# A two-layer encoder on one core: bias expanded within the second stage, one weight sum on VectorE, token sums in the slot freed last

## The chip, the core and the metric

The kernel runs on one core of a Trainium2 chip. Its engines are TensorE (PE; its weight loads are shown apart, as PEld), VectorE (DVE), ScalarE (ACT), GpSimd (POOL) and SyncE (SP), which here issues nearly all DMAs. The metric is the device time of one execution in microseconds; before the change it is 1210.97 us, the median of 3 runs (1210.27 to 1211.98).

## The reference

An encoder trunk of two layers over 512 tokens (8 rows of 64) of width 1024, all in float32. Each layer is an attention and a squared-ReLU MLP with 4096 hidden columns, with a normalisation ahead of each; a last normalisation ends it. The first layer's attention is a hybrid of two kinds; the second's looks at a neighbourhood of 8 x 16 positions and adds a learned bias by relative position. What the change touches:

```
def sq_relu_mlp(h, w_up, w_down):
    u = jax.nn.relu(h @ w_up)
    return (u * u) @ w_down

# in neighbourhood_attention, for a block of 128 queries:
bias = rpb[:, rblk, cblk].astype(jnp.float32)
sc = jnp.einsum('bhqd,bhqkd->bhqk', qblk, kg).astype(jnp.float32) * scale + bias[None]
```

## The kernel before

**Precision.** A float32 factor is split into a high part (rounded by a copy to a narrower float type, on ACT) and a low part (what is left, by a subtraction on DVE). A product is three matmuls: high by high, high by low, low by high.

**The MLP of layer 0** (`mlp`, L1201 on) goes through the 32 tiles of 128 hidden columns in three stages, z = 0, 1, 2: up product of some tiles, squared ReLU, then down product of these tiles, added to the residual `hT` (L1199). The first 6 hidden tiles are made by a plain up product. The rest are made *by sevens* (class `Seven`): two by two blocks of weights and of tokens are multiplied with seven products in place of eight, from sums and differences of blocks. The last 12 tiles of the third stage are kept raw, without a split, as their down product is done by sevens as well (`u7`): it needs sums of token blocks (`Seven.sums`, L325 to L327 on POOL) and splits of these sums (`Seven.split`, L348 on ACT and L349 on DVE). These run, a step at a time, between the matmuls of the third stage's plain down product. `u7` then makes four groups of two output tiles (L1226 adds each to `hT`), with six weight chunks each.

**A weight chunk by sevens** (`seven_chunk`, L289 on) is a 128 x 1024 tile `raw` with four blocks loaded by one DMA of SP (L292), 256 KB. POOL forms three more: L294 (one block of 128 x 128), L295 (two) and L296 (one, from an output of L295). ACT makes the high parts of seven blocks (L299, `whi`) and DVE the low parts (L300, `wlo`). PE then does 21 matmuls (L373 to L375). There are four `raw` buffers and three each of `whi` and `wlo`. At the end of a pair of output tiles L382 to L385 put the sums together on DVE. Layer 0 has 76 such chunks: 16 in the second stage, 36 in the third (the last 24 for the twelve raw tiles) and 24 in `u7`. Plain products have weight chunks of their own (`chunk`), with L211 on ACT and L201 on DVE.

**The order of the work.** Chunks are asked for by `plan` and made by `weights`, two ahead of the one that PE works on (`AHEAD = 2`). In the attention the order of the instructions is written out by hand; in the MLP a scheduler orders each engine's instructions as the program is built, and each engine, SP's queue of DMAs among them, then runs its own in that order, waiting where an operand is late.

**Slots.** Token tiles live in a fixed set of 128 x 1024 slots (class `Slot`, L65); a new one takes the slot at the head of the list of free ones, and a slot that is given up goes to its end.

**The bias** (L1236 to L1258) stands behind `mlp(0)` in the source. Eight small DMAs bring the rows of the table into the slot R (L1242); POOL fills and copies them into Fi and Fe (L1244 to L1248); 48 DMAs of 64 or 128 KB write the expanded bias to DRAM (`bx`, L1251, L1254 and L1255). Layer 1's attention reads it back.

Of the kernel before, what the change touches and what calls it, by code (L numbers as in the profile page):

```python
# [8 lines left out]
F32 = mybir.dt.float32  # L9
F32R = mybir.dt.float32r  # L10
I32 = mybir.dt.int32
AF = mybir.ActivationFunctionType
ALU = mybir.AluOpType
# [5 lines left out]
P = 128  # L19
# [3 lines left out]
NEG = -1e30  # L23
# [12 lines left out]
def encoder_kernel(ctx: ExitStack, tc: tile.TileContext, ins, out, dbg=None):  # L36
    nc = tc.nc
    PE, ACT, DVE, POOL, SP = nc.tensor, nc.scalar, nc.vector, nc.gpsimd, nc.sync
# [7 lines left out]
    dr = ctx.enter_context(tc.tile_pool(name="dr", bufs=1, space=bass.MemoryType.DRAM))  # L46
# [16 lines left out]
        return f"{s}_{cnt[0]}"  # L63

    class Slot:  # L65
        def __init__(self, dt=F32R):
            self.i = take()[0]
            self.t = big.tile([P, 1024], dt, tag=f"a{self.i}", name=nm("a"))

# [162 lines left out]
    def plan(*spec, make=None):  # L232
        asked.append((make or chunk, spec))
        return len(asked) - 1
# [51 lines left out]

    SEVEN = [(0, 0), (2, 2), (4, 5), (3, 3), (5, 4), (6, 1), (1, 6)]

    def seven_chunk(w, k0, c0):  # L289

        raw = wp.tile([P, 1024], F32, tag="raw", bufs=4, name=nm("raw"))
        SP.dma_start(raw[:, 0:512].rearrange("p (k n) -> p k n", k=2), rows(w, k0, 2)[:, :, c0 : c0 + 256])  # L292
        r = raw.rearrange("p (b n) -> p b n", n=P)
        POOL.tensor_tensor(r[:, 6], r[:, 0], r[:, 1], op=ALU.subtract)  # L294
        POOL.tensor_tensor(r[:, 4:6], r[:, 2:3].to_broadcast([P, 2, P]), r[:, 0:7:6], op=ALU.add)  # L295
        POOL.tensor_tensor(r[:, 7], r[:, 3], r[:, 5], op=ALU.subtract)  # L296
        hi = wp.tile([P, 1024], F32R, tag="whi", name=nm("whi"))
        lo = wp.tile([P, 1024], F32R, tag="wlo", name=nm("wlo"))
        ACT.activation(hi[:, 0:896], raw[:, 128:1024], AF.Copy)  # L299
        return hi, lo, [lambda: DVE.tensor_tensor(lo[:, 0:896], raw[:, 128:1024], f32(hi[:, 0:896]),  # L300
                                                  op=ALU.subtract)]

    class Seven:
# [13 lines left out]
            q = self.number(kp, b)  # L317
            return self.slots[q // 2].t.rearrange("p (q z n) -> p q z n", q=2, z=2)[:, q % 2]

        def sums(self, kp, raw):  # L320

            t = Slot(F32)
            self.raw[kp] = raw, t
            r, t_ = (s_.t.rearrange("p (b n) -> p b n", n=256) for s_ in (raw, t))
            POOL.tensor_tensor(t_[:, 0:2], r[:, 0:1].to_broadcast([P, 2, 256]), r[:, 1:3], op=ALU.subtract)  # L325
            POOL.tensor_tensor(t_[:, 2], r[:, 2], t_[:, 0], op=ALU.subtract)
            POOL.tensor_tensor(t_[:, 3], r[:, 3], t_[:, 2], op=ALU.subtract)  # L327
# [27 lines left out]
            for s_ in self.slots.values():  # L355
                s_.free()

        def plan(self, w, c0, k0=0):
            return [plan(w, k0 + 2 * kp, c0, make=seven_chunk) for kp in range(self.np)]

        def run(self, ids, evac):

# [726 lines left out]
    def first_product(l):  # L1089

        w = ins["ffn_w_up"][l]
        X = [Slot() for _ in range(KD)]
        acc = pp.tile([P, S], F32, tag="p", name=nm("acc"))
        for k in range(KD):
            split_g(hT[:, k, :], gffn(l, k), X[k].pair())
            sumsq_acc(k, acc, DVE)
        xp = [s_.pair() for s_ in X]
        U, R = [], []
        rb = keep([P, S], F32, "rb")
        state = dict(c=SIZES[l][0], ids=None, plain=False)  # L1100
        x7 = Seven(KD)

        def ev(j, b):
            U.append(Slot())
            t = scratch()
            DVE.scalar_tensor_tensor(t, b, 0.0, rb, op0=ALU.max, op1=ALU.mult)
            uu = scratch()
            ACT.activation(uu, t, AF.Square)
            split(uu, U[-1].pair())

        def norm():
            r = compact_r(acc)
            bk = stb()
            bcast_cols(lambda i: r[:, i : i + 1].to_broadcast([P, P]), P, bk)
            ACT.activation(rb, bk, AF.Copy)

        def x_sums(kp):
            raw = Slot(F32)
            for z in range(2):
                k = 2 * kp + z  # L1120
                DVE.scalar_tensor_tensor(raw.t[:, S * z : S * z + S], hT[:, k, :], gffn(l, k), rb, op0=ALU.mult,
                                         op1=ALU.mult)
            x7.sums(kp, raw)

        def raw_evac(w_):
            ACT.activation(w_.t, w_.t, AF.Relu)
            ACT.activation(w_.t, w_.t, AF.Square)
            R.append(w_)
            return True

        def pair_evac(w_):
            raw_evac(w_)
            R.pop()
            for z in range(2):
                U.append(Slot())
                split(w_.t[:, S * z : S * z + S], U[-1].pair())

        def plain():
            four = product(w, 0, xp, tiles(0, 512), ev, lambda n: [mmb(), mmb(), mmb(), sbk()])
            two = product(w, 0, xp, tiles(512, 256), ev, lambda n: [sbk(), ob()], kstep=4)  # L1140
            for n, _ in enumerate(four):
                if n == (11 if l == 0 else 13):
                    norm()
                if n == 14:
                    x_sums(0)
                    x_sums(1)
            for n, _ in enumerate(two):
                if n == 4:
                    x_sums(2)
                if n == 6:  # L1150
                    x_sums(3)
            flip[0] = 1
            for s_ in X:
                s_.free()
            state["plain"] = True

        def later(c, n):

            if (c, n) in ((0, 2), (0, 10), (0, 18), (1, 4)):
                x7.split({(0, 2): 0, (0, 10): 1, (0, 18): 2, (1, 4): 3}[c, n])  # L1160

        def ahead():
            state["ids"] = x7.plan(w, P * state["c"])

        def stage(n, raw=0):

            if not state["plain"]:
                plain()
            left = n + raw - len(U)
            while left:  # L1170
                i = state["ids"]
                state["c"] += 2
                left -= 2
                if left:
                    ahead()
                for _ in x7.run(i, pair_evac if left >= raw else raw_evac):
                    pass
            if state["c"] == 32:
                x7.free()
            got = list(U), list(R)  # L1180
            U.clear()
            R.clear()
            return got

        return stage, ahead, later

    def mlp(l):


        stage, ahead, later = first_product(l)  # L1190
        w = ins["ffn_w_down"][l]
        k0 = 0
        for z, n in enumerate(SIZES[l][:3]):
            raw = SIZES[l][3] if z == 2 else 0
# [7 lines left out]
            k0 += n  # L1202
            if raw:
                u7 = Seven(raw)
                ids = [u7.plan(w, 256 * m, k0) for m in range(4)]
                u7.sums(0, R[0])
            else:
                ahead()
            every = 8 * n // u7.np if raw else 0
            for c, gen in enumerate(gens):  # L1210
                for i, _ in enumerate(gen):
                    if z == 0:
                        later(c, i)
                    if raw:
                        kp, at = divmod(4 * n * c + i, every)
                        if at == 0 and kp + 1 < u7.np:
                            u7.sums(kp + 1, R[kp + 1])
                        if at == 2 and kp < u7.np:
                            u7.split(kp)
            for s_ in U:  # L1220
# [10 lines left out]

    mlp(0)

    bx = dr.tile([16, 2, P, 256], F32, name="bx")  # L1236
    R = Slot(F32)
    Fi = Slot(F32)
    Fe = Slot(F32)
    rpb = ins["od_rpb"][0]  # L1240
    for qr in range(8):
        SP.dma_start(R.t[16 * qr : 16 * qr + 16, 0:248],  # L1242
                       rpb.rearrange("h a b -> h (a b)")[:, (7 - qr) * 31 : (7 - qr) * 31 + 248])
    POOL.memset(Fi.t[:, 0:376], NEG)  # L1244
    POOL.memset(Fe.t[:, 256:512], NEG)
    rv = R.t[:, 0:248].rearrange("p (k d) -> p d k", d=31)
    POOL.tensor_copy(Fi.t[:, 0:376].rearrange("p (j k) -> p j k", k=8)[:, 15:31, :], rv[:, 7:23, :])
    POOL.tensor_copy(Fe.t[:, 0:248].rearrange("p (j k) -> p j k", k=8), rv)  # L1248
    bxv = bx.rearrange("h t (c r) k -> t c r h k", r=8)
    for c in range(16):  # L1250
        SP.dma_start(bxv[0, c].rearrange("r h k -> r h k"), Fi.t[:, (15 - c) * 8 : (15 - c) * 8 + 256])  # L1251

        v, off = (1, (7 - c) * 8) if c < 8 else (0, (23 - c) * 8)
        SP.dma_start(bxv[1, c][:, :, 128 * v : 128 * v + 128], Fe.t[:, off : off + 128])  # L1254
        SP.dma_start(bxv[1, c][:, :, 128 - 128 * v : 256 - 128 * v], Fe.t[:, 256:384])  # L1255
    R.free()
    Fi.free()
    Fe.free()  # L1258

    X = [Slot() for _ in range(KD)]  # L1260
    acc = pp.tile([P, S], F32, tag="p", name=nm("acc"))
# [423 lines left out]
```

## Time and profile before

| what | value |
| --- | --- |
| median of 3 runs | 1210.97 us (1210.27 to 1211.98) |
| the profiled execution | 1210.45 us |
| its span | 1208.7 us |
| mean granted PE clock | 0.995 |
| DMA packets, MB | 108511, 127.99 |
| mean DMA rate | 106 GB/s |

The span is the time from the first to the last instruction in the profile; the rest of the execution's time lies around it. A group line of the profile names line, engine, operation and tiles, then the number of instructions, their busy time in us and the mean of one in ns, then the time that the engine sat idle just ahead of them and what ended it. A row of the timeline has the start and the duration in us, and in brackets the wait ahead of it and its releaser. A row of a window has its bounds and length, the busy time and number of instructions of each engine, the granted PE clock as a share of the full one, the busy share of the DMA engines and GB/s.

### The profile page before, as it was taken

To read this page: it belongs to the slowest core of one execution; us is meant where nothing else is said; L and a number is where in the kernel's file an instruction comes from. 1 tells how busy PE (TensorE), PEld (TensorE's weight loads), DVE (VectorE), ACT (ScalarE), POOL (GpSimd) and SP (SyncE) were. 2 spreads that over 40 slices of the span, in tenths; PEclk is the share of its full clock that TensorE was granted. 3 is DMA by queue.
4 is the path that set the end of the run, shared out by engine and by line. 5 is a ranking of instruction groups with operands and counts; after the bars stand their busy time and mean duration, and the time that the engine had idled before them with its cause. 6 is when DMAs were issued, how large, how long until landed. Compare 5 with 4: busy or idle time off the path is not lost.

```text
span 1208.7 us, 19500 instructions
## 1 busy us (share of the span) xinstructions
PE 1174.6 (97%) x7020; PEld 1018.2 (84%) x7020; DVE 841.7 (70%) x1447; ACT 629.8 (52%) x1065; POOL 514.1 (43%) x641
## 2 busy tenths in 40 slices
PE   9999999999999999998999999999999999999997
PEld 7667788887898898877998988988878988988985
DVE  4588988878666477794885675767984753664764
ACT  4577677755355156562443555655463642551553
POOL 3257252205472389974941232221343903723800
PEclk9999999999999999999999999999999999999999
DMA  7223314212234133324655564433222341341432
GB/s 239 72 57 90 84 54 130 70 53 77 72 96 149 46 99 94 116 85 131 188 149 145 157 162 133 128 100 121 88 79 62 105 157 44 92 153 44 123 123 69
DMA packets 108511, 127.99 MB, mean 106 GB/s; under 512 B 8979, under 2 KB 83648, under 8 KB 108416
## 3 DMA queue, kind: packets, MB, share of 16 engines
q1 hardware_dynamic: 105360, 119.30, 33.7%
q0 software_dynamic: 2304, 6.31, 2.3%
q10 hardware_dynamic: 752, 1.15, 0.4%
q8 instruction: 55, 0.90, 0.3%
q14 instruction: 40, 0.33, 0.1%
HBM read 104.32 MB, written 6.29 MB: 92 GB/s over the span
## 4 chain that ended last, share of the span: by engine, by line
PE 75%; DVE 8%; POOL 6%; ACT 4%; issue 3%; DMA 2%; SPq 1%; POOLq 0%; DVEq 0%; ACTq 0%
PE mm L486 7%; PE mm L488 7%; PE mm L487 7%; PE s L976 2%; PE o L964 2%; POOL raw L295 2%; PE mm L375 2%; PE mm L373 2%; PE mm L374 2%; PE s L488 2%; PE s L486 2%; PE t L951 2%; PE s L487 2%; PE mm L1583 2%; PE mm L1585 2%
## 5 line engine op out<-in xcount | busy, mean ns | idle before, releaser
L300 DVE TENSOR_TENSOR wlo<-raw,whi 128x896 fp32r<-128x896 f32 x128 | 160.8, 1256 | 122.5 <-ACT whi L299 120.2
L299 ACT ACTIVATE whi<-raw 128x896 fp32r<-128x896 f32 x128 | 121.6, 950 | 199.3 <-POOL raw L296 63.0
L201 DVE TENSOR_TENSOR wlo<-raw,whi 128x1024 fp32r<-128x1024 f32 (+4 forms) x123 | 144.9, 1182 | 97.3 <-ACT whi L211 97.0
L211 ACT ACTIVATE whi<-raw 128x1024 fp32r<-128x1024 f32 (+3 forms) x126 | 122.6, 974 | 126.4 <-PE o L1585 30.6
L294 POOL TENSOR_TENSOR raw<-raw 128x128 f32<-128x128 f32 x128 | 84.3, 659 | 231.4 <-DMA raw<-in_ffn_w_up_dram 153.7
L486 PE MATMUL mm<-a,whi 128*128 128x512 f32 x419 | 169.4, 406 | 0.2 <-DVE hT L910 0.2
L487 PE MATMUL mm<-a,whi 128*128 128x512 f32 x419 | 165.9, 396 | 0.0
L488 PE MATMUL mm<-a,wlo 128*128 128x512 f32 x419 | 165.7, 397 | 0.0
L295 POOL TENSOR_TENSOR raw<-raw 128x256 f32<-128x256 f32 x128 | 120.5, 942 | 10.0
L296 POOL TENSOR_TENSOR raw<-raw 128x128 f32<-128x128 f32 x128 | 105.8, 827 | 10.0
L375 PE MATMUL mm<-a,wlo 128*128 128x256 f32 x340 | 97.9, 288 | 4.7 <-DVE wlo L300 4.6
L373 PE MATMUL mm<-a,whi 128*128 128x256 f32 x340 | 96.5, 284 | 5.4 <-ACT whi L299 5.4
L374 PE MATMUL mm<-a,whi 128*128 128x256 f32 x340 | 96.2, 283 | 0.0
L488 PEld LDWEIGHTS mm<-a,wlo 128*128 128x128 f32 x419 | 78.5, 188 | 19.7 <-issue 1.7
L486 PEld LDWEIGHTS mm<-a,whi 128*128 128x128 f32 x419 | 78.7, 188 | 17.3 <-issue 1.9
L487 PEld LDWEIGHTS mm<-a,whi 128*128 128x128 f32 x419 | 78.9, 188 | 16.3 <-issue 1.7
L984 POOL TENSOR_SCALAR p<-p,ti 128x512 f32<-128x512 f32 x64 | 46.3, 725 | 88.2 <-DVE ti L983 74.0
L1386 POOL TENSOR_SCALAR p<-p,ti 128x256 f32<-128x256 f32 x64 | 35.6, 567 | 105.1 <-DVE ti L1385 92.0
L375 PEld LDWEIGHTS mm<-a,wlo 128*128 128x128 f32 x340 | 65.0, 191 | 7.0 <-DVE wlo L300 6.7
L373 PEld LDWEIGHTS mm<-a,whi 128*128 128x128 f32 x340 | 65.1, 192 | 6.0 <-ACT whi L299 5.8
L374 PE MATMUL t<-a,whi 128*128 128x256 f32 x240 | 67.4, 281 | 0.0
L375 PE MATMUL t<-a,wlo 128*128 128x256 f32 x240 | 67.3, 280 | 0.0
(325 smaller groups left out, 3284.9 us busy)
## 6 DMA issues: line engine op xcount, KB each, us to landing
raw<-in_ffn_w_down_dram SPq DMA_DIRECT2D x52, 512.0 KB
raw<-in_ffn_w_up_dram SPq DMA_DIRECT2D x104, 256.0 KB
raw<-in_od_w_qkv_dram SPq DMA_DIRECT2D x64, 128.0 KB
raw<-in_ffn_w_up_dram SPq DMA_DIRECT2D x12, 512.0 KB
raw<-in_ffn_w_down_dram SPq DMA_DIRECT2D x24, 256.0 KB
raw<-in_ev_w_in_dram SPq DMA_DIRECT2D x12, 384.0 KB
a<-a SPq DMA_DIRECT2D x18, 256.0 KB
bias<-bx SPq DMA_DIRECT2D x16, 256.0 KB
```

The lines of the kernel that those rows point to most:

```text
L201: z = lambda: (eng or DVE).tensor_tensor(to, src, f32(high), op=ALU.subtract)
L211: ACT.activation(hi[:, 0:m], raw[:, 0:m], AF.Copy)
L295: POOL.tensor_tensor(r[:, 4:6], r[:, 2:3].to_broadcast([P, 2, P]), r[:, 0:7:6], op=ALU.add)
L296: POOL.tensor_tensor(r[:, 7], r[:, 3], r[:, 5], op=ALU.subtract)
L299: ACT.activation(hi[:, 0:896], raw[:, 128:1024], AF.Copy)
L300: return hi, lo, [lambda: DVE.tensor_tensor(lo[:, 0:896], raw[:, 128:1024], f32(hi[:, 0:896]), op=ALU.subtract)]
L373: PE.matmul(o, wh, x[:, 0], start=kp == 0 and n in (0, 1, 3, 5), stop=False, skip_group_check=True)
L374: PE.matmul(o, wh, x[:, 1], start=False, stop=False, skip_group_check=True)
L375: PE.matmul(o, wl, x[:, 0], start=False, stop=kp == self.np - 1, skip_group_check=True)
L486: PE.matmul(o, wh, xh, start=first, stop=False)
L487: PE.matmul(o, wh, xl, start=False, stop=False)
L488: PE.matmul(o, wl, xh, start=False, stop=last)
```

## The change

Three edits. First, the bias code becomes a generator, `bias_rows`, with a `yield` behind each DMA and six behind the copies; `mlp` takes one step of it at each step of the second stage's plain down product (z = 1). The scheduler still orders the instructions. Second, `seven_chunk` is told the engine of its last sum: DVE for the chunks of the twelve raw tiles and for all of `u7`, 48 in all, and POOL for the others. Third, the slots for the token sums of `u7` are taken from the end of the free list, that is, the one given up last.

```
     class Slot:
-        def __init__(self, dt=F32R):
+        def __init__(self, dt=F32R, last=False):
+            if last:
+                free.insert(0, free.pop())
...
-    def seven_chunk(w, k0, c0):
+    def seven_chunk(w, k0, c0, last=None):
...
-        POOL.tensor_tensor(r[:, 7], r[:, 3], r[:, 5], op=ALU.subtract)
+        (last or POOL).tensor_tensor(r[:, 7], r[:, 3], r[:, 5], op=ALU.subtract)
...
-        def sums(self, kp, raw):
+        def sums(self, kp, raw, late=False):
...
-            t = Slot(F32)
+            t = Slot(F32, late)
...
-        def plan(self, w, c0, k0=0):
-            return [plan(w, k0 + 2 * kp, c0, make=seven_chunk) for kp in range(self.np)]
+        def plan(self, w, c0, k0=0, last=None):
+            return [plan(w, k0 + 2 * kp, c0, last, make=seven_chunk) for kp in range(self.np)]
...
-                    ahead()
+                    ahead(DVE if left <= raw else None)
...
+    def bias_rows():
+        R, Fi, Fe = Slot(F32), Slot(F32), Slot(F32)
+        rpb = ins["od_rpb"][0]
+        for qr in range(8):
+            SP.dma_start(R.t[16 * qr : 16 * qr + 16, 0:248],
+                           rpb.rearrange("h a b -> h (a b)")[:, (7 - qr) * 31 : (7 - qr) * 31 + 248])
+            yield
+        POOL.memset(Fi.t[:, 0:376], NEG)
+        POOL.memset(Fe.t[:, 256:512], NEG)
+        rv = R.t[:, 0:248].rearrange("p (k d) -> p d k", d=31)
+        POOL.tensor_copy(Fi.t[:, 0:376].rearrange("p (j k) -> p j k", k=8)[:, 15:31, :], rv[:, 7:23, :])
+        POOL.tensor_copy(Fe.t[:, 0:248].rearrange("p (j k) -> p j k", k=8), rv)
+        for _ in range(6):
+            yield
+        bxv = bx.rearrange("h t (c r) k -> t c r h k", r=8)
+        for c in range(16):
+            SP.dma_start(bxv[0, c].rearrange("r h k -> r h k"), Fi.t[:, (15 - c) * 8 : (15 - c) * 8 + 256])
+            yield
+            v, off = (1, (7 - c) * 8) if c < 8 else (0, (23 - c) * 8)
+            SP.dma_start(bxv[1, c][:, :, 128 * v : 128 * v + 128], Fe.t[:, off : off + 128])
+            yield
+            SP.dma_start(bxv[1, c][:, :, 128 - 128 * v : 256 - 128 * v], Fe.t[:, 256:384])
+            yield
+        for s_ in (R, Fi, Fe):
+            s_.free()
+        yield
...
+        bias = bias_rows()
...
-                ids = [u7.plan(w, 256 * m, k0) for m in range(4)]
-                u7.sums(0, R[0])
+                ids = [u7.plan(w, 256 * m, k0, DVE) for m in range(4)]
+                u7.sums(0, R[0], True)
...
+                    if z == 1:
+                        next(bias, None)
...
-                            u7.sums(kp + 1, R[kp + 1])
+                            u7.sums(kp + 1, R[kp + 1], True)
...
     mlp(0)
-    bx = dr.tile([16, 2, P, 256], F32, name="bx")
-    R = Slot(F32)
-    Fi = Slot(F32)
-    Fe = Slot(F32)
...
```

More of the change, by code (lines that the diff above doesn't have):

```diff
@@ L1160, in later, with ahead @@
                 x7.split({(0, 2): 0, (0, 10): 1, (0, 18): 2, (1, 4): 3}[c, n])
-        def ahead():
-            state["ids"] = x7.plan(w, P * state["c"])
+        def ahead(last=None):
+            state["ids"] = x7.plan(w, P * state["c"], last=last)
         def stage(n, raw=0):
@@ L1185, in first_product @@
         return stage, ahead, later
+    bx = dr.tile([16, 2, P, 256], F32, name="bx")
+    def bias_rows():
[24 more added lines that the diff above has]
+        yield
     def mlp(l):
@@ L1232, in encoder_kernel @@
     mlp(0)
-    bx = dr.tile([16, 2, P, 256], F32, name="bx")
-    R = Slot(F32)
-    Fi = Slot(F32)
-    Fe = Slot(F32)
[L1240 to L1258, printed above, removed]
     X = [Slot() for _ in range(KD)]
```

## The prediction

> **What bounds the kernel now.** I read the head of the page first: who is busy, and what the chain that ended last is made of; then the largest groups of VectorE (DVE), ScalarE (ACT) and GpSimd (POOL) that the change touches.
>
> ```profile
> span 1208.7 us, 19500 instructions
> PE 1174.6 (97%) x7020; PEld 1018.2 (84%) x7020; DVE 841.7 (70%) x1447; ACT 629.8 (52%) x1065; POOL 514.1 (43%) x641
> ...
> PE 75%; DVE 8%; POOL 6%; ACT 4%; issue 3%; DMA 2%; SPq 1%; POOLq 0%; DVEq 0%; ACTq 0%
> ...
> L300 DVE TENSOR_TENSOR wlo<-raw,whi 128x896 fp32r<-128x896 f32 x128 | 160.8, 1256 | 122.5 <-ACT whi L299 120.2
> L299 ACT ACTIVATE whi<-raw 128x896 fp32r<-128x896 f32 x128 | 121.6, 950 | 199.3 <-POOL raw L296 63.0
> ...
> L294 POOL TENSOR_TENSOR raw<-raw 128x128 f32<-128x128 f32 x128 | 84.3, 659 | 231.4 <-DMA raw<-in_ffn_w_up_dram 153.7
> ...
> L295 POOL TENSOR_TENSOR raw<-raw 128x256 f32<-128x256 f32 x128 | 120.5, 942 | 10.0
> L296 POOL TENSOR_TENSOR raw<-raw 128x128 f32<-128x128 f32 x128 | 105.8, 827 | 10.0
> ```
>
> TensorE (PE) is busy 97% of the span and makes 75% of the chain, so only time in which PE waits can be won or lost. The span-wide shares hide where. The busy time by stage shows it; I cut where PE changes from one product to the next: the first product by sevens of the second stage (z = 1), its plain product, the first product by sevens of the third stage (z = 2), its plain product, and the last product by sevens with the w_down weights, up to its last matmul. I number the seven-chunks of this layer 1 to 76: 1-16 are in the first row, 17-52 in the third (29-52 make the twelve tiles that stay raw), 53-76 in the fifth.
>
> ```profile
> core 0: us, PE busy (x) PEld busy (x) DVE busy (x) ACT busy (x) POOL busy (x), PEclk, DMA share, GB/s
> 334.89:374.49 39.60, 39.60 (x337) 39.59 (x336) 29.01 (x32) 23.77 (x30) 26.78 (x32) 1.00 0.41 120
> 374.49:419.50 45.01, 45.01 (x195) 35.93 (x194) 21.05 (x25) 12.77 (x15) 10.76 (x17) 1.00 0.26 83
> 419.50:517.44 97.94, 92.25 (x757) 89.93 (x756) 73.15 (x79) 57.31 (x73) 86.83 (x103) 1.00 0.35 102
> 517.44:551.63 34.19, 33.79 (x147) 26.96 (x145) 32.56 (x38) 16.90 (x28) 21.11 (x21) 1.00 0.27 77
> 551.63:624.21 72.58, 64.05 (x506) 62.76 (x504) 51.56 (x51) 30.27 (x39) 53.30 (x65) 0.95 0.54 160
> ```
>
> The first row has no gap: 39.60 us for 16 chunks is 2.475 us a chunk. By that, 36 chunks take 89.1 us and the third row loses 8.8; 24 take 59.4 and the fifth loses 13.2. The plain product of 144 matmuls at 45.01/192 = 0.234 us would take 33.8; the fourth row loses 0.4. So 22.4 us lie in these stages for a change to win. In the third row POOL is busy 89%; in the fourth DVE is, with only 34.19 - 32.56 = 1.63 us idle. What PE waited for in the sevens, over the whole run, and the one large stall of the fifth row:
>
> ```profile
> PE mm L373 <- ACT whi L299: 5.4, 2, 4.1
> PE s L375 <- DVE wlo L300: 4.6, 5, 1.3
> PE mm L375 <- DVE wlo L300: 4.6, 8, 0.8
> ```
> ```profile
> 570.74 0.39 PE L373 MATMUL mm<-a,whi 128*128 128x256 f32 x1 [4.05 <-ACT whi L299]
> ```
> ```profile
> 572.00:578.00 6.00, 6.00 (x28) 6.00 (x29) 3.95 (x4) 2.17 (x3) 5.14 (x8) 0.50 0.70 219
> ```
>
> The 4.05 us come from SP: the bias writes stand in its queue between two weight loads, and the later load lands late. Behind the stall the granted clock is 0.50 for 6 us, which costs another 3 us.
>
> ```profile
> 556.92 0.40 SPq L292 DMA_DIRECT2D raw<-in_ffn_w_down_dram  x1
> 557.74 0.59 SPq L1251 DMA_DIRECT2D bx<-a  x1
> 558.45 0.57 SPq L1254 DMA_DIRECT2D bx<-a  x1
> ...
> 564.09 0.41 SPq L292 DMA_DIRECT2D raw<-in_ffn_w_down_dram  x1
> ```
> ```profile
> 567.92 0.46 POOL L294 TENSOR_TENSOR raw<-raw 128x128 f32<-128x128 f32 x1 [6.27 <-DMA raw<-in_ffn_w_down_dram]
> ```
>
> **Part one: the bias.** The rows for it are those of the bias loads (four in a row), of the matmul that reads last from the slot they will get, and of the load and the low part of chunk 6:
>
> ```profile
> 545.51 1.84 SPq L1242 DMA_DIRECT2D a<-in_od_rpb_dram  x4
> ```
> ```profile
> 329.06 0.39 PE L488 MATMUL o<-a,wlo 128*128 128x512 f32 x1
> ```
> ```profile
> 331.42 0.37 SPq L292 DMA_DIRECT2D raw<-in_ffn_w_up_dram  x1
> ```
> ```profile
> 343.45 1.28 DVE L300 TENSOR_TENSOR wlo<-raw,whi 128x896 fp32r<-128x896 f32 x1 [1.23 <-ACT whi L299]
> ```
>
> All of it leaves the fifth stage: 8 loads, 48 writes, two fills and two copies. What it adds earlier is not what its place in the source says. SP runs its queue in order and meets the writes by the order that the scheduler gave it: the 8 loads come behind chunk 5's weight load, and 44 of the 48 writes stand three to eight at a time between the loads of chunks 6 to 16 and those of the next stage, so they are issued in the first row's product by sevens, not in the plain product behind it. A load there leaves SP every 3 to 4 x 0.62 (the spacing of the writes above) + 0.41 = 2.3 to 2.9 us, against 2.475 that PE takes. Chunk 6's load moves from 331.4 to about 333.4, as PE reads the slot for the bias rows until 329.4 and 8 loads at 0.46 us go ahead. Its low part began 12.0 us behind its load, more than the load, the sums and both parts need in themselves (about 6.9 by the ring of part two, with ACT's 0.95), so 2 us at the start are covered; from there each gap of over 2.475 eats at that lead. Working it chunk by chunk I get a lateness of at most 1 us at chunks 7 to 10: **+0.8 us** (0 to +1.5). Without the lead, eleven gaps that are up to 0.4 us too long would cost 4. What is won in the fifth stage is in part four.
>
> **Part two: the weight sum on DVE, chunks 29 to 52.** For 48 chunks the third sum leaves POOL (0.83 us each by L296's group) for DVE. DVE's order has it directly ahead of the low part (L300) of the chunk two before. DVE prices for a 128x128 subtract do not stand in the trace; its nearest rows:
>
> ```profile
> L661 DVE SCALAR_TENSOR_TENSOR a<-t,r,a 128x128 fp32r<-128x128 f32 x4 | 1.4, 350 | 2.1 <-ACT a L660 2.0
> L384 DVE TENSOR_TENSOR a<-a,mm 128x256 f32<-128x256 f32 x16 | 6.6, 411 | 0.0
> L1301 DVE SCALAR_TENSOR_TENSOR sc<-mm,rb 128x64 f32<-128x64 f32 x8 | 1.7, 213 | 0.0
> ```
>
> Between 0.21 (half as wide) and 0.41 (twice as wide); I take 0.30, nearest to the 0.35 of the row of that width with one operand more. 48 x 0.30 is 14 us of DVE work, and 40 us leave POOL. The work matters less than the wait. DVE runs in order, so the low part of chunk k now waits for the load and two POOL sums of chunk k+2; and that load waits for one of four raw buffers, which the low part of chunk k-2 frees. That closes a ring, and one turn of it can be read from a place where the load was the last to come:
>
> ```profile
> 338.49 1.09 DVE L300 TENSOR_TENSOR wlo<-raw,whi 128x896 fp32r<-128x896 f32 x1 [1.34 <-ACT whi L299]
> ```
> ```profile
> 342.50 0.47 POOL L294 TENSOR_TENSOR raw<-raw 128x128 f32<-128x128 f32 x1
> 343.05 0.74 POOL L295 TENSOR_TENSOR raw<-raw 128x256 f32<-128x256 f32 x1
> ```
>
> The low part ends at 339.58, the second sum of the chunk loaded into its buffer at 343.79: 4.21 us. With 0.30 for the sum and about 1.2 for the next low part, 5.7 us for two chunks, where PE takes 4.95. In the third row DVE also has the evacuation of each pair of tiles, L382 to L385, of which L384 stands above and the three others are like this:
>
> ```profile
> L383 DVE TENSOR_TENSOR a<-a,mm 128x512 f32<-128x512 f32 x16 | 11.0, 687 | 1.6
> ```
>
> That is 2.5 us of DVE for four chunks, some of it between a sum and a low part; a count turn by turn gives 11.8 us for four chunks (two turns of 5.7 and 0.4) where PE needs 9.9, but the queue starts with a lead and POOL's relief returns up to the 8.8 us lost now. My count ends the stage at 519.3 instead of 517.44: **+1.9** (-3 to +5).
>
> A rule weighed: the Trainium skill, "SBUF — State Buffer", section "SBUF: two separate sides", says that DVE with two SBUF inputs and GpSimd reading SBUF hold a shared port exclusively, the later one waiting for the whole instruction. The trace agrees in kind: L294 has 0.47 in the row above and 0.659 in its group's mean. By the rule each moved sum is one more holder against POOL, though in the ring POOL is done when it starts; if half of 48 met a POOL sum of 0.74 us, another 17 us would go to waits, most of them off PE's path.
>
> **Part three: token sums and the plain product of the third stage.** The slots for the token sums (L325 to L327) are now those that came free last; PE reads them until the last chunk by sevens.
>
> ```profile
> L325 POOL TENSOR_TENSOR a<-a 128x512 f32<-128x512 f32 x14 | 24.7, 1764 | 73.8 <-DVE a L1121 73.8
> L326 POOL TENSOR_TENSOR a<-a,a 128x256 f32<-128x256 f32 x14 | 16.9, 1209 | 1.1
> L327 POOL TENSOR_TENSOR a<-a,a 128x256 f32<-128x256 f32 x14 | 15.9, 1139 | 1.1
> ```
>
> 4.1 us a tile, and all six, three of which ran in the third stage before, now fall into the plain product, each waiting for the split two before: 24.6 us of POOL in 34. Chunk 54's weight sums stand behind the sixth, and DVE's third sum for 54 stands ahead of the plain product's fifth weight low part. In a stage where DVE has 1.63 us of idle time, it waits about 2.5 us for chunk 53 and 4.6 for chunk 54; PE wants the fifth low part 23 us into the stage and has it at about 27, with a further one for the sixth: **+5** (+1, if the sums run at their uncontended best, to +6).
>
> **Part four: the last product by sevens.** Gone: 4.05 us and 3 us of clock. New: the low parts of chunks 54 and 55 stand behind the sums of 57 and 58, whose loads wait for the buffers that these very turns free: a turn each, less what PE had in hand, 3.3 and 3.9 us by my count. Then each group of six chunks is three turns, 17.1 us, and the part of the evacuation and of the residual's addition that stands between a sum and a low part, for which I take one such addition:
>
> ```profile
> L1226 DVE TENSOR_TENSOR hT<-hT,a 128x1024 f32<-128x1024 f32 x4 | 5.9, 1475 | 0.1
> ```
>
> 18.6 us a group, where PE needs 14.85. The four groups and the two stalls are 81.6 us, less about 1.5 by which the first turn begins ahead of the stage: 80.1 for 72.58, **+7.5** (+4, if each group hides its L1226, to +10).
>
> The sum: 0.8 + 1.9 + 5 + 7.5 = +15.2 on the profiled execution's 1210.45 us (span 1208.7): 1225.7. The median of the three runs, 1210.97, is 0.5 above it: **1226**. The bounds of the terms that are least sure together give 1215 to 1232.
>
> **The rivals.**
> *Faster (0.20):* DVE's waits fall where it sat idle anyway (122.5 us ahead of L300, by its group), PE never sees them, and what goes is the 5.4 of L373's waits, half of the 9.2 of the two L375 waits as POOL is relieved, and 3 us of clock, less 0.8 for the bias: -12.2, or **1199**. It decides at one number: whether a turn for two chunks is under PE's 4.95 us. For it speaks that POOL's three sums weigh more than 2.4 us a chunk by their groups; against it, the 4.21 us between the two rows of the ring, in which POOL has only 1.2.
> *Gains and losses cancel (0.08):* the plain product hides the waits and the turns cost 0.3 us a chunk: **1211**.
> *The change does not do what its first part says (0.05):* the bias, meant for a plain product with 45 us and a DMA share of 0.26, collides with loads at a share of 0.41, and each of the 44 writes delays a load by its 0.62 less the slack of 2.475 - 0.41 a chunk: some 5 us in the first row instead of 0.8: **1230**.
> *Worse by the clock (0.07):* the stalls at chunks 54 and 55 are as long as the 4.05 that the granted clock of 0.50 followed; twice 3 us, and more of the ring's waits at half speed: **1234**. The Trainium skill, "TensorE: Matmul & The Clock Gate", section "What's actually happening", puts the point at one idle window of about 3.4 us; the trace agrees with one stall of 4.05. By it the stall of 3.9 would halve the clock and that of 3.3 would not.
>
> **How the numbers follow.** The forecast has 0.60. Faster by over 0.2% (2.4 us, about what a measurement of this kernel can tell from no change) 0.20, within it 0.08, slower 0.60 + 0.05 + 0.07 = 0.72. The range of 8 in 10 takes the forecast's own 1215 to 1232 and reaches down through the cancelling case to 1203, leaving out most of the faster one, and up to 1233, leaving out most of the worst.
>
> **What would show it.** Right: DVE idle ahead of the new sum and ended by POOL or a DMA; PE waiting for L300's low part at chunks 54 and 55, over 3 us each; the five stages at about 40.4, 45, 99.8, 39.2 and 80 us; POOL's busy time some 40 us lower; no bias write in the fifth stage. Wrong: low parts of the fifth stage closer than 2.6 us in the mean; the plain product at 34; weight loads of the fifth stage issued without waiting for a low part.

## The result, and the profile after

The changed kernel takes 1229.31 us (median of 4 runs, 1228.61 to 1230.46), the kernel before 1210.62 beside it (4 runs, 1210.18 to 1211.98): a ratio of 1.0153, 95% interval 1.0136 to 1.0171, so 18.7 us slower. The forecast was 1226.

The head of the page after, with the same rows as before; L303 is the old L300, L302 the old L299, L297 to L299 the old L294 to L296:

```profile
span 1226.8 us, 19535 instructions
...
PE 1178.8 (96%) x7020; PEld 1018.9 (83%) x7020; DVE 842.9 (69%) x1495; ACT 630.0 (51%) x1065; POOL 459.3 (37%) x593
...
PE 71%; DVE 13%; ACT 4%; issue 4%; DMA 4%; POOL 4%; SPq 1%; DVEq 0%; POOLq 0%; ACTq 0%
```

POOL lost 54.8 us of busy time and DVE gained 1.2, yet DVE's share of the chain rose from 8 to 13%. An engine that is hardly busier and holds the end up more often is one that others wait for while it waits itself. DVE's groups by shape say for whom:

```profile
L303 DVE TENSOR_TENSOR wlo<-raw,whi 128x896 fp32r<-128x896 f32 x128 | 152.3, 1190 | 87.3 <-ACT whi L302 82.7 <-PE t L378 2.7 <-DMA raw<-in_ffn_w_up_dram 1.5
...
L299 DVE TENSOR_TENSOR raw<-raw 128x128 f32<-128x128 f32 x48 | 16.3, 339 | 55.0 <-POOL raw L298 54.6
```

The moved sum costs 0.339 us each, 16.3 in all, and DVE stands 55.0 us ahead of it waiting for POOL's second sum. The low part's own wait fell from 122.5 to 87.3. The same five stages as before:

```profile
333.36:376.08 42.72, 40.90 (x337) 39.94 (x336) 28.84 (x32) 23.66 (x30) 27.37 (x34) 1.00 0.67 197
376.08:421.25 45.17, 45.03 (x195) 35.93 (x193) 21.42 (x25) 12.92 (x15) 9.71 (x16) 1.00 0.32 103
421.25:519.96 98.71, 93.12 (x757) 90.21 (x756) 70.43 (x103) 56.32 (x72) 51.32 (x70) 1.00 0.34 100
519.96:562.70 42.74, 35.79 (x147) 27.89 (x146) 34.83 (x38) 18.42 (x28) 26.46 (x26) 0.96 0.17 54
562.70:643.12 80.42, 64.43 (x506) 61.93 (x504) 53.06 (x76) 30.53 (x40) 30.40 (x40) 0.98 0.29 89
```

| stage | before | after | change | forecast |
| --- | --- | --- | --- | --- |
| z = 1, by sevens | 39.60 | 42.72 | +3.1 | +0.8 |
| z = 1, plain | 45.01 | 45.17 | +0.2 | 0 |
| z = 2, by sevens | 97.94 | 98.71 | +0.8 | +1.9 |
| z = 2, plain | 34.19 | 42.74 | +8.5 | +5 |
| last, by sevens | 72.58 | 80.42 | +7.8 | +7.5 |

They add to +20.4; the part ahead is 1.5 us shorter (its length is between 332.5 and 334.9 in all profiles here, and no edit but that of the fifth raw buffer touches it) and the part behind 0.8, which leaves the span's 18.1. In the last stage one turn of the ring can be read off; SP, POOL and DVE:

```profile
579.94 0.37 SPq L295 DMA_DIRECT2D raw<-in_ffn_w_down_dram  x1
```
```profile
582.80 0.46 POOL L297 TENSOR_TENSOR raw<-raw 128x128 f32<-128x128 f32 x1 [2.30 <-DMA raw<-in_ffn_w_down_dram]
583.34 0.74 POOL L298 TENSOR_TENSOR raw<-raw 128x256 f32<-128x256 f32 x1
```
```profile
578.56 1.35 DVE L303 TENSOR_TENSOR wlo<-raw,whi 128x896 fp32r<-128x896 f32 x1
...
584.11 0.29 DVE L299 TENSOR_TENSOR raw<-raw 128x128 f32<-128x128 f32 x1 [2.29 <-POOL raw L298]
584.32 1.09 DVE L303 TENSOR_TENSOR wlo<-raw,whi 128x896 fp32r<-128x896 f32 x1
```

Chunk 57's low part ends at 579.91; 0.03 us later the load of chunk 61 leaves SP into its buffer; POOL waits for it and ends its two sums at 584.08; DVE, which has waited 2.29 us, makes the sum, and only then chunk 59's low part, to 585.41. From low part to low part 5.50 us for two chunks, where PE needs 4.95. PE's waits in the last stage:

```profile
PE s L378 <- DVE wlo L303: 10.4, 5, 3.3
PE mm L378 <- DVE wlo L303: 5.6, 6, 2.0
```

### The profile page after: what moved, and what is told of

Its sections match the earlier page's. It is cut to its first block, busy times and chain, and to the rows that moved or that the text cites. A ratio compares the mean times of both kernels' runs of the same rounds, so it can differ in the third digit from the quotient of the medians.

```text
span 1226.8 us, 19535 instructions
## 1 busy us (share of the span) xinstructions
PE 1178.8 (96%) x7020; PEld 1018.9 (83%) x7020; DVE 842.9 (69%) x1495; ACT 630.0 (51%) x1065; POOL 459.3 (37%) x593
## 4 chain that ended last, share of the span: by engine, by line
PE 71%; DVE 13%; ACT 4%; issue 4%; DMA 4%; POOL 4%; SPq 1%; DVEq 0%; POOLq 0%; ACTq 0%
PE mm L491 7%; PE mm L489 7%; PE mm L490 7%; DVE wlo L303 3%; PE s L979 2%; PE o L967 2%; DMA raw<-in_ffn_w_down_dram 2%; PE mm L378 2%; PE t L954 2%; PE mm L1597 2%; PE mm L1598 2%; PE mm L1596 2%; DMA raw<-in_ffn_w_up_dram 2%; DVE wlo L203 2%; PE mm L376 1%
## 5 line engine op out<-in xcount | busy, mean ns | idle before, releaser
L302 ACT ACTIVATE whi<-raw 128x896 fp32r<-128x896 f32 x128 | 121.0, 948 | 187.5 <-PE o L377 29.8
L303 DVE TENSOR_TENSOR wlo<-raw,whi 128x896 fp32r<-128x896 f32 x128 | 152.3, 1190 | 87.3 <-ACT whi L302 82.7
L297 POOL TENSOR_TENSOR raw<-raw 128x128 f32<-128x128 f32 x128 | 81.8, 639 | 292.5 <-DMA raw<-in_ffn_w_up_dram 192.6
L298 POOL TENSOR_TENSOR raw<-raw 128x256 f32<-128x256 f32 x128 | 110.0, 859 | 9.9
L378 PE MATMUL mm<-a,wlo 128*128 128x256 f32 x340 | 97.7, 287 | 10.1 <-DVE wlo L303 9.9
L489 PEld LDWEIGHTS mm<-a,whi 128*128 128x128 f32 x419 | 79.1, 189 | 17.3 <-issue 1.4
L490 PEld LDWEIGHTS mm<-a,whi 128*128 128x128 f32 x419 | 79.2, 189 | 16.7 <-issue 1.7
L378 PE MATMUL s<-a,wlo 128*128 128x256 f32 x196 | 57.0, 291 | 12.8 <-DVE wlo L303 12.7
L376 PE MATMUL t<-a,whi 128*128 128x256 f32 x240 | 67.9, 283 | 0.0
L377 PE MATMUL t<-a,whi 128*128 128x256 f32 x240 | 67.9, 283 | 0.0
```

The lines of the kernel that those rows point to most:

```text
L376: PE.matmul(o, wh, x[:, 0], start=kp == 0 and n in (0, 1, 3, 5), stop=False, skip_group_check=True)
L377: PE.matmul(o, wh, x[:, 1], start=False, stop=False, skip_group_check=True)
L378: PE.matmul(o, wl, x[:, 0], start=False, stop=kp == self.np - 1, skip_group_check=True)
L489: PE.matmul(o, wh, xh, start=first, stop=False)
L490: PE.matmul(o, wh, xl, start=False, stop=False)
```

## The experiments

The theory: the loss is DVE's waiting in order for the sum of chunk k+2 ahead of the low part of chunk k. Rivals: A, the token sums that all fall into the third stage's plain product; B, the work that DVE got, or what it shares with POOL; C, too few raw buffers. Edits are against the changed kernel unless said otherwise; each ratio is to runs of the kernel before on the same chip.

**Each edit alone, and the change without its second edit.** The first three kernels keep one edit each; the fourth is this:

```
-                    ahead(DVE if left <= raw else None)
+                    ahead()
-                ids = [u7.plan(w, 256 * m, k0, DVE) for m in range(4)]
+                ids = [u7.plan(w, 256 * m, k0) for m in range(4)]
```

The bias alone has that and `True` taken from both calls of `u7.sums`. The sums on VectorE alone and the token slots alone are the kernel before with that edit.

> Only the first edit: the bias expanded by steps in the second stage's plain product; all weight sums on GpSimd, token sums in the slot at the head of the list. By the traces of before and after, the first product by sevens should take 42.7 us as in after (+3.1), since the writes still stand between its weight loads, and the last product by sevens should lose its 4.05 us stall and the half clock behind it: 72.6 - 7 = about 65.5. Theory (the loss of after comes from the VectorE sums' place): 1206 to 1207. Rival (moving the bias costs more than it brings): 1211 or more.

> Only the second edit: the last weight sum of chunks 29 to 76 on VectorE; the bias stays behind the MLP and the token sums keep their old slots. Theory (VectorE waits in order for a sum that stands ahead of an earlier chunk's low part): the plain product of the third stage grows by 4 to 8 us and the last product by sevens is again near 80 us, where the bias writes add a little: 1224 to 1230. Rival A (the plain product's loss comes from the token sums that all fall into it): the plain product stays within 1.5 us of 34.2, and the total is 1217 to 1220.

> Only the third edit: token sums in the slot freed last. Theory (VectorE's waits for weight sums make the loss): the plain product of the third stage grows by at most 2 us and the total is 1210 to 1213. Rival A (six token sums in the plain product make its loss): the plain product grows by 5 to 9 us, total 1216 to 1220.

> First and third edit, that is, after with all weight sums back on GpSimd. Theory: the sum of both single edits, 1206 to 1209, with the third stage's plain product under 36.5 us and the last product by sevens at 65 to 68. Rival A: the plain product stays at 40 us or more, total 1213 to 1216.

| kernel | median us | ratio (95%) | five stages, us |
| --- | --- | --- | --- |
| bias alone | 1203.79 | 0.9954 (0.9939 to 0.9969) | 42.9, 45.1, 98.8, 34.2, 63.8 |
| VectorE sums alone | 1225.8 | 1.0140 (1.0125 to 1.0155) | 39.6, 44.9, 104.9, 33.5, 81.5 |
| token slots alone | 1209.19 | 0.9997 (0.9988 to 1.0006) | 39.6, 44.8, 91.7, 40.4, 73.1 |
| without VectorE sums | 1203.18 | 0.9949 (0.9933 to 0.9966) | 41.7, 45.2, 92.0, 40.8, 63.7 |

Two of three edits do no harm; the second turns a gain of 0.5% into a loss of 1.5%, some 25 us. The bias alone came out 2 us below what I wrote (its last product takes 63.8 us, where I had 65.5), and the kernel without VectorE's sums below both sides: its plain product is rival A's, its total is not. The second edit also costs elsewhere than I had it. With VectorE's sums alone, the plain product is not longer at all, where I expected 4 to 8 us. The rows of that kernel for the third and fourth stage:

```profile
418.46:523.36 104.90, 93.68 (x758) 90.27 (x757) 77.44 (x104) 57.61 (x74) 64.40 (x81) 1.00 0.31 95
523.36:556.88 33.52, 33.52 (x147) 27.04 (x145) 27.39 (x37) 16.58 (x27) 16.66 (x15) 1.00 0.26 79
```

The token slots alone make the plain product 6.2 us longer, as rival A has it, and take 6.3 us off the product by sevens ahead of it, which neither side had written down; hence no change in total. In the rows of that kernel POOL is 10.1 us less busy in the third stage and 12.4 more in the fourth. There ACT now waits 16.5 us for the token sums (L327 to L329 here) with the high parts of the splits (L350), which it did not before. DVE runs in order, so a weight low part that stands behind the split low parts comes late as well:

```profile
418.55:510.20 91.65, 90.55 (x757) 89.45 (x756) 69.70 (x79) 57.04 (x73) 76.71 (x93) 1.00 0.36 110
510.20:550.63 40.43, 35.73 (x147) 27.95 (x145) 34.89 (x38) 17.80 (x27) 33.55 (x32) 0.96 0.22 63
```
```profile
ACT a L350 <- POOL a L329: 12.0, 5, 4.0
ACT a L350 <- POOL a L327: 4.5, 3, 1.9
PE mm L490 <- DVE wlo L203: 3.2, 1, 3.2
PE mm L488 <- ACT whi L213: 1.5, 1, 1.5
```

PE waits 4.7 us in that stage, and is busy 35.73 us where it was 33.79, as the granted clock is 0.50 for 3.4 us behind the longer wait.

Of the plain product's +8.5 in the changed kernel, 6.6 are there without any sum on VectorE (40.80), and 1.9 are the sums. Against the kernel without them, VectorE's sums cost 6.7 us in the third stage's product by sevens, 1.9 in its plain product and 16.7 in the last product; 23.4 of the 25 us are where the ring stands. Alone they cost 8.9 in the last product (81.48 for 72.58). In the kernel before, that stage has its own stall by the bias writes; that DVE's waits run beside it there is how I read the difference, and no run shows it apart.

**The sums stay on VectorE, the ring is opened.** A copy of one column from the low part of the chunk two before into the place of the sum (which overwrites it) keeps the sum of chunk k+2 behind the low part of chunk k:

```
+    los = []
...
+        if last:
+            DVE.tensor_copy(r[:, 7, 0:1], f32(los[-2][:, 0:1]))
         (last or POOL).tensor_tensor(r[:, 7], r[:, 3], r[:, 5], op=ALU.subtract)
...
+        los.append(lo)
```

> The changed kernel with one tiny VectorE copy ahead of each moved sum: it reads a column of the low part of the chunk two before, so that the sum of chunk k+2 can't stand ahead of the low part of chunk k. The 48 sums stay on VectorE, and 48 copies of one column are added. Theory (the loss is the ring of load, sum, low part): the third stage's product by sevens goes to 92 to 94, the last one from 80.4 to 63 to 67: 1204 to 1212. Rival B (VectorE's added work, or what it shares with GpSimd, is the loss): no gain, 1226 or more.

1212.91 us, ratio 1.0028 (1.0018 to 1.0037). The two products by sevens, and DVE's groups by shape (L303 is the sum here, L302 the copy):

```profile
421.58:514.36 92.78, 90.68 (x758) 89.55 (x756) 78.07 (x127) 56.56 (x73) 56.91 (x69) 1.00 0.35 109
514.36:562.34 47.98, 38.30 (x146) 30.01 (x145) 38.05 (x46) 17.96 (x27) 29.32 (x30) 0.86 0.17 55
562.34:626.10 63.76, 61.35 (x506) 60.01 (x504) 57.37 (x92) 30.64 (x40) 27.15 (x37) 1.00 0.34 104
```
```profile
L303 DVE TENSOR_TENSOR raw<-raw 128x128 f32<-128x128 f32 x48 | 18.6, 390 | 2.4 <-POOL raw L300 0.6
...
L302 DVE COPY raw<-wlo 128x1 f32<-128x1 f32 x48 | 6.8, 146 | 0.5
```

This settles it between the theory and rival B. DVE does all the sums and 48 copies more, is busier in the last stage (57.37 us against 53.06), and the stage takes 63.76 us, not 80.42: the same as with the sums on POOL (63.7). DVE's wait ahead of the sum fell from 55.0 us to 2.4. So in the products by sevens it was the wait, and neither the work nor anything shared. The total is 0.9 us above what I wrote, and still some 9.6 us (by the two ratios) above the kernel without VectorE's sums, as the plain product grew to 47.98: there two weight low parts stand behind low parts of the token splits. PE waited 6.3 us for the first and 3.4 us for the second, which stood behind eight of them, 10.57 us.

**Five raw buffers.** `bufs=5` for `raw`, and one buffer less in the pools `scp` and `pp` to make room:

> The changed kernel with five raw buffers in place of four (and one buffer less in two pools of 128x512 tiles that make room for it). The scheduler then puts the sum of chunk k+3, not k+2, ahead of the low part of chunk k. Theory: the ring still closes over two chunks, so the last product by sevens stays at 78 to 82 us and the total within 4 us of the changed kernel. Rival C (too few raw buffers are the bound by themselves): the last product by sevens falls to 70 or less, total under 1220.

1220.57 us, ratio 1.0090 (1.0072 to 1.0108). The last product takes 80.31 us, as the theory has it: a buffer more and a sum a chunk earlier close the same ring. Its turn, from chunk 57's low part to chunk 59's, is 5.44 us (5.50 in the changed kernel). PE waits 11.7 us there and not 16.0, but its mean granted clock is 0.92 and not 0.98. Rival C falls for this stage. The total is some 8 us below the changed kernel's, more than the 4 I allowed, and that comes from other stages: 40.43 us in the first (against 42.72) and 40.37 in the plain product (against 42.74). The fifth buffer lets loads run further ahead (the first load of the last product leaves SP 3.0 us into the plain product, and 8.9 in the changed kernel); that this is what shortens those stages is only likely.

**One group of sums at a time.** VectorE's sums only for chunks 29 to 52, or only for the last product (the second hunk of the first diff alone, and the first hunk alone):

> The changed kernel with VectorE's sums only in chunks 29 to 52 and GpSimd's in the last product by sevens. Theory (the ring costs by the stage in which it stands): the third stage's product by sevens as in the changed kernel, 98 to 99, the last one 63 to 65 and the plain product near 41: 1208 to 1212. If VectorE's sums for chunks 53 to 56 within the plain product made that product's loss, it falls to 36 or less and the total to 1204 to 1207.

> The changed kernel with VectorE's sums only in the last product by sevens. Theory: the third stage's product by sevens at 92, its plain product at 42 to 43, the last product at 79 to 82: 1219 to 1224. Rival (the two groups of sums only hurt together): under 1215.

1212.1 us, ratio 1.0020 (1.0011 to 1.0030), with 100.0, 41.8 and 64.0 us in the last three stages; and 1221.46 us, ratio 1.0101 (1.0086 to 1.0116), with 92.5, 42.2 and 81.2. Each group costs in its own stage, and the plain product stays near 42 us in both, so the sums of chunks 53 to 56 are not what makes it long. The second is within what the theory gave, the first at its upper edge.

**The bias where the source has it.** Against the first edit alone, the first hunk, and then all three:

```
-        R, Fi, Fe = Slot(F32), Slot(F32), Slot(F32)
+        R, Fi, Fe = Slot(F32, True), Slot(F32), Slot(F32)
...
-        POOL.memset(Fe.t[:, 256:512], NEG)
+        POOL.memset(R.t[:, 256:512], NEG)
...
-            SP.dma_start(bxv[1, c][:, :, 128 - 128 * v : 256 - 128 * v], Fe.t[:, 256:384])
+            SP.dma_start(bxv[1, c][:, :, 128 - 128 * v : 256 - 128 * v], R.t[:, 256:384])
```

> First edit alone, with one difference: the slot for the bias rows is the one freed last, so that the rows can't be loaded before the first product by sevens of the second stage is over and the writes fall into the plain product, where the source has them. Theory (the +3.1 us of that product by sevens are the writes between its weight loads): it goes back to 39.6 us, the plain product of 45 us grows by less than 1, the last product by sevens stays at 63.8: 1200 to 1202. Rival (the writes cost as much wherever they stand ahead of weight loads): 1203 to 1205, with the plain product at 47 to 48.

> As the kernel with the bias rows in the slot freed last, and the constant part of the bias is written from that slot too, so that all 48 writes fall into the plain product of the second stage. Theory: the first product by sevens of that stage goes to 39.6 (from 42.5 with 16 of the writes ahead of it), the plain product stays within 1 us of 45.0: 1198.5 to 1200.5. Rival (those 2.9 us are not the writes): 1201 to 1203.

The first has the lowest median of all here: 1201.97 us, ratio 0.9936 (0.9919 to 0.9952). Its total is within what the theory gave, but partly by luck, as one of its stages is not: the constant third of the writes, which needs no rows, still stood at the start of the first product by sevens, which took 42.5 us and not 39.6; the other 32 went into the plain product, and it took 45.0, against the rival's 47 to 48. In the second all 48 go there, and its first two stages are as I wrote, 39.60 and 44.88. Its total is neither side's: 1207.54 us, ratio 0.9988 (0.9978 to 0.9998). The next product by sevens, the third row, takes 105.35 us:

```profile
334.19:373.79 39.60, 39.60 (x338) 39.60 (x336) 28.96 (x32) 23.94 (x30) 26.73 (x32) 1.00 0.38 120
373.79:418.67 44.88, 44.88 (x195) 35.93 (x194) 17.22 (x22) 11.68 (x14) 3.01 (x6) 1.00 0.48 144
418.67:524.02 105.35, 95.60 (x757) 92.05 (x756) 75.52 (x84) 58.22 (x74) 95.08 (x116) 0.98 0.38 114
```
```profile
410.19 0.57 SPq L1210 DMA_DIRECT2D bx<-a  x1
410.86 0.41 SPq L295 DMA_DIRECT2D raw<-in_ffn_w_up_dram  x1
411.32 0.59 SPq L1214 DMA_DIRECT2D bx<-a  x1
```

Its first weight load leaves SP at 410.86 behind 34 writes, 8 us ahead of the stage; in the changed kernel it left at 389.98, and the stage began with five chunks loaded and summed. In the kernel with 32 writes there the first load leaves at 391.74, ahead of them, and the third row takes 97.6 us. The stock that the plain product used to build is gone, and where POOL is busy 95 of 105 us it isn't made up. The start is shown (between 418 and 430 us PE is busy 8.84 of 12); that the other half of the +6.6 us against the bias alone follows from it is only argued.

**Two candidates for a faster kernel.** One has the bias rows in the slot freed last, both groups of sums on VectorE with the copy of one column, and the token sums in their old slots; the other is the kernel with all 48 writes in the plain product, with this:

```
-                            u7.sums(kp + 1, R[kp + 1])
+                            u7.sums(kp + 1, R[kp + 1], True)
```

> Candidate for a faster kernel: the bias as in the kernel with its rows in the slot freed last, the moved sums on VectorE with the tying copies, token sums in their old slots. Theory: the third stage's product by sevens at 94 to 98 and its plain product near 34, the last product by sevens at 60 to 64: 1194 to 1201. Rival B: 1215 or more.

> As the last kernel, and the token sums but the first in the slot freed last. Theory (the token sums cost PE about 6 us whether they run in the product by sevens or in the plain product, as a bound engine stands in each): within 2 us of the last kernel. If the split between the two stages hides part of them, 1194 to 1197.

1206.03 us, ratio 0.9970 (0.9959 to 0.9981), with 98.3, 38.3 and 63.6 us in the last three stages, and 1205.13 us, ratio 0.9966 (0.9954 to 0.9978), with 102.3, 35.3 and 63.2. The first is slower than I wrote: taking the sum off POOL brings nothing in the third stage as long as token sums stay in it (98.3 against 97.6), where taking the token sums out of it does (92.0 without VectorE's sums). So it is not the third weight sum on POOL that costs time there. The second is 2.4 us below the kernel it was made from, 3.0 less in the third stage's product by sevens and 1.1 more in its plain product: just enough to be told apart, and far from the 1194 to 1197 of a division that hides them. The three fastest kernels, with the bias rows late (1201.97), without VectorE's sums (1203.18) and with the bias alone (1203.79), can't be told apart by their intervals.

## Why the prediction was right, and where it was not

**The sum** was 15.2 us where 18.7 were measured; the sign, the ring and the last stage stand. By its steps:

**Part one, the bias.** The reading that the writes leave SP between the weight loads of the product by sevens was right: with none there it takes 39.60 us, with them 42.72. The size was not: +3.1 for +0.8. I priced SP's queue and not the transfers beside it. SP and POOL of the changed kernel at chunk 10:

```profile
347.48 0.40 SPq L295 DMA_DIRECT2D raw<-in_ffn_w_up_dram  x1
```
```profile
352.46 0.87 POOL L297 TENSOR_TENSOR raw<-raw 128x128 f32<-128x128 f32 x1 [1.56 <-DMA raw<-in_ffn_w_up_dram]
```

From issue to POOL 4.98 us where the ring's row had 2.89, while the DMA engines are 0.67 busy, 0.41 before, as they carry the writes too. The load also leaves SP 4.2 us later against the start of its stage than before (14.1 us for 9.9); that part I had roughly, with 2 us at chunk 6 and up to 0.4 a gap. What a given number of writes costs there varies, though: 16 at the start of the stage went with +2.9 in one kernel and +0.4 in another with the same writes (42.5 and 40.0). The two weight loads among the writes leave SP 2.2 us later against the start of the stage in the first; why is left open. The rival that priced the collision at 5 us was the nearer one.

**Part two, the ring.** 0.30 us for a 128x128 subtract, measured 0.339, and 0.28 to 0.29 where POOL doesn't run beside it. A turn of 5.7 us, measured 5.50. The stage's +1.9 came out at +0.8, but as the difference of two larger terms of which I had one too small and missed the other: the sums cost 6.7 to 7 us there, and the third edit takes 6.3 off. The step that failed is that "POOL's relief returns up to the 8.8 us": what was lost there came from the token sums ahead of the weight sums, not from the third weight sum.

**The Trainium skill's rule** ("SBUF — State Buffer", section "SBUF: two separate sides") that DVE and GpSimd lock each other out: the trace agrees in kind, as some moved sums took 0.80 us beside a POOL sum and 0.28 alone. It carries next to nothing of the loss in the products by sevens, since the opened ring keeps every sum on DVE and takes 92.78 and 63.76 us there, for 91.99 and 63.70 with the sums on POOL. (24 waits of 0.74 us, which I weighed there, are 17.8 us and not 17.)

**Part three, the plain product.** +8.5 for +5, and most of it by another road than the one I named. The step that failed is "it waits about 2.5 us for chunk 53 and 4.6 for chunk 54". DVE of the changed kernel, and then of the kernel before at the same place:

```profile
535.01 0.81 DVE L299 TENSOR_TENSOR raw<-raw 128x128 f32<-128x128 f32 x1 [1.75 <-POOL raw L298]
...
539.14 7.56 DVE L352 TENSOR_TENSOR a<-a,a 128x512 fp32r<-128x512 f32 x7
548.41 0.80 DVE L299 TENSOR_TENSOR raw<-raw 128x128 f32<-128x128 f32 x1 [1.71 <-POOL raw L298]
549.13 1.21 DVE L203 TENSOR_TENSOR wlo<-raw,whi 128x1024 fp32r<-128x1024 f32 x1
```
```profile
531.08 7.30 DVE L349 TENSOR_TENSOR a<-a,a 128x512 fp32r<-128x512 f32 x7
538.30 1.21 DVE L201 TENSOR_TENSOR wlo<-raw,whi 128x1024 fp32r<-128x1024 f32 x1
```

The waits are 1.75 and 1.71 us. With the two sums they make 5.1 of the 8.3 us by which the fifth weight low part begins later into its stage (29.2 us, 20.9 before); PE waited 5.3 us for it. But take every sum off VectorE, and that low part still begins 25.7 us into the stage, and the stage is still 6.2 to 6.6 us longer. The splits have not become more: 19 of their low parts fall into the stage in both kernels, and seven stand in a row ahead of the fifth weight low part in both. They come later, because their high parts wait on ACT for the token sums (16.5 us with the token slots alone, 13.1 in the changed kernel). I had counted POOL's 24.6 us of token sums for this stage, and had only the weight sums wait for them, not the splits, whose low parts stand ahead of the weight low parts on DVE. The third term is the clock, which I had at nothing in this stage: behind the 5.3 us it is 0.50 for 3.4 us, and PE is busy 35.79 us for 33.79.

**Part four, the last product.** +7.8 for +7.5, with the parts as told: 63.8 us once the bias is out (8.8 gained, where I had 4.05 and 3 of clock), and 16.7 for the ring and its two stalls. PE waited 2.57 and 3.31 us at chunks 54 and 55, for 3.3 and 3.9; the three groups of six chunks behind chunk 58, low part to low part, took 19.6, 20.3 and 18.8 us, for 18.6.

**The rivals.** Faster by relief of POOL: its test was a turn under 4.95 us, and it was 5.50. Worse by the clock: it did fall, less than priced; PE after the second stall, with the granted clock behind it:

```profile
574.20 0.58 PE L378 MATMUL s<-a,wlo 128*128 128x256 f32 x1 [3.31 <-DVE wlo L303]
```
```profile
574.00:578.00 4.00, 3.80 (x19) 3.80 (x20) 1.15 (x2) 0.00 (x0) 0.89 (x2) 0.57 0.40 131
```

Four us at 0.57 cost 1.7, and the fall in the plain product as much again; I had priced twice 3 us, both in the last product.

## What to carry to other kernels

An operation moved to an idle engine takes that engine's order with it: look at what is queued behind it, and whether its operand waits for something that this queue frees; a ring of load, sum and low part costs by its length over its chunks. Here a fifth buffer did not open it, and one dependency that turned the order round did, though it added work. An opened ring is not yet a gain: the changed kernel with it, 1212.91 us, was no faster than the one before. When work moves between stages, follow all that waits for it (here the high parts and low parts of the splits, and a weight low part queued behind them), and not only the engine that does it, and credit the stage it leaves. A plain product that seems to have room for DMAs may be the one that builds the next stage's stock of weights.

## What the runs showed of the hardware

A stall of 3.31 us was enough for the granted clock to fall to 0.50 (0.57 over the next four us), after one of 2.57 behind which it stayed at 1.00. The length of the stall alone does not decide it. With five raw buffers a stall of 2.07 us was enough; with VectorE's sums only in the last product one of 2.77 was not:

```profile
602.83 0.54 PE L378 MATMUL s<-a,wlo 128*128 128x256 f32 x1 [2.07 <-DVE wlo L303]
```
```profile
603.00:606.00 3.00, 3.00 (x15) 3.00 (x16) 2.94 (x6) 0.00 (x0) 0.68 (x2) 0.50 0.29 90
```
```profile
561.60 0.38 PE L378 MATMUL s<-a,wlo 128*128 128x256 f32 x1 [2.77 <-DVE wlo L303]
```
```profile
562.00:566.00 4.00, 2.36 (x20) 2.15 (x19) 1.61 (x5) 0.95 (x1) 1.18 (x2) 1.00 0.19 66
```

The falls, read in windows of 0.1 us, last 3.4 us or a multiple of it: 574.2 to 577.7 and 550.3 to 553.8 in the changed kernel, 602.9 to 606.4 with five raw buffers, 571.2 to 578.1 in the kernel before. The Trainium skill, "TensorE: Matmul & The Clock Gate", section "What's actually happening", puts the window at about 3.4 us and says that it runs free of the program. The trace agrees with that length. It does not agree with a stall of a whole window as the condition, by which I had judged 3.3 and 3.9: 3.31 was on the other side from where I had put it, and 2.07 is well short of it.

A VectorE copy of one column costs 0.146 us, half of a 128x128 subtract.
